# Attention probabilities transposed in 32x32 blocks by VectorE, with 32-row value products

## The chip, the cores and the metric

One Trainium2 chip, one of its cores. The core has TensorE (matmuls, PE in the profile; its weight loads are PEld), VectorE (DVE), ScalarE (ACT), GpSimd (POOL) and SyncE (SP, which only starts transfers). Each engine works through its own queue in order and waits on semaphores. The metric is the device time of one execution in microseconds, the median of several runs; less is better.

## What is computed

One layer of an encoder on 512 positions of width 1024: a gated feed-forward half step, a mixing step, a second feed-forward half step, and a last norm. The change lies in the mixing step:

```
h = rms_norm(x, mix_norm);  u = h @ w_in        # 512 fourier | 8x64 q | 2x64 k | 2x64 v
A = real(fft2(fourier group)) @ fnet_w + fnet_b # per group of 128 channels
q, k = rms_norm per head, then axial rotary
p = softmax(q @ k.T / 8)                        # 4 query heads share one k, v head
B = p @ v
x = x + concat([A, B]) @ w_out
```

All values are float32. The kernel gets this precision from TensorE's faster format (fp32r) by splitting each operand into a high part (a rounded copy) and a low part (value minus high part), and adds three products: high x high, high x low, low x high (`product`, L163 to L166).

## The kernel before

Activations lie with channels on partitions and the 512 positions along the free axis, in 8 tiles of 128x512. The mixing stage is written as some 600 small named operations (`op`), and one long list, `ORDER`, says in which order they are issued; each engine's queue is the list's operations that fall to it. The names that matter here, with t = 0..3 the query pair, b = 0, 1 the key/value head, c a block of 128 queries, kc a block of 128 keys:

- `w*.r/.h/.l`, `f*.`, `fw.`, `o*.`: a weight tile is loaded by SyncE (r), ScalarE makes its high part (h, L858) and VectorE its low part (l, L123, `lows`). f0 to f3 belong to the Fourier projection, o0 to o7 to the output projection. `HI_DVE` names those whose high part VectorE makes (f0, f1).
- `k.0..7`, `q0.0..7`, `v.0..7`: steps of the projections, three 512-column products each; `n1.*` is the row scale of the norm (L233; n1.t turns it on TensorE), `.rc/.rs` the rotary, `.pq/.s0/.s1/.s2` the per-head scale in `sc` (s1 on GpSimd, L949).
- `s{t}{b}{c}` scores (L1188, L1189), `m` the row maximum by a reduce and a multiply on VectorE (L1194, L1195), `e` the exponentials on ScalarE with their row sum (L1202).
- `t{t}{b}{kc}` turns the probabilities: four 128x128 transposes on TensorE into one PSUM bank (L1214). `h` (ScalarE, L1219) and `l` (VectorE, L123) split the bank into high and low part, tiles ph and pl. `v` multiplies them with the values (L1257, tile `vst`: high and low part of v side by side, 128 columns). The rows of high and low part are then added (`o.c` L1267 on ScalarE, `o.a` L1272 on VectorE).
- `z.r/.w/.p` invert the row sums, spread them (GpSimd, L1239) and turn them on TensorE; `r.m/.h/.l` scale the result and split it. `y{d}.0..7` are the eight steps of output block d; k = 0..3 take the Fourier part, k = 4..7 the attention part.
- `f{h}{c}.`, `d`, `c`, `map`: the Fourier mixer.

PSUM has 8 banks of 128x512. In the mixing stage `bank_for` hands them out in turn, and `read` gives one back after its last reader.

Of the kernel before, what the change touches and what calls it, by code (L numbers as in the profile page):

```python
# [13 lines left out]
P = 128  # L14
# [23 lines left out]
HI_DVE = ("f0", "f1")  # L38
# [5 lines left out]
wk.r wq0.r wv.r cos wk.h wk.l wq0.h k.0 k.1 k.2 k.3 k.4 wv.h k.5 wq0.l k.6 wq1.r k.7 k.sq q0.0 wq1.h n1.c  # L44
k.rc n1.m k.sw n1.p q0.1 q0.2 q0.3 q0.4 wq1.l q0.5 wq2.r n1.t q0.6 q0.7 wq2.h q1.0 k.rs k.pq wv.l q0.sw
n1.b v.0 v.1 k.s0 k.s1 wq2.l q0.rc f2.r wq3.r q0.rs q0.ah q0.bh k.s2 v.2 kw v.3 v.4 v.5 v.6 q0.sq q0.al
q0.bl v.7 vt kp wq3.h km q1.1 wq3.l q0.pq f0.r q0.s0 k1.0 k0.0 k0.1 q1.2 q1.3 q1.4 q1.5 k1.2 k0.2 vp q1.6
q1.7 k0.3 s003 s001 s000 k1.1 k1.3 s010 f1.r v0.h v0.l q0.s1 q0.s2 f0.h m001 m003 s002 q1.sw m002 m010 q1.sq
q1.sd q1.pq e002 m000 v1.h e000 e001 e003 q2.0 q2.1 q2.2 q1.s0 q1.s1 f0.l q1.rc q1.rs v1.l q2.3 q2.4 q1.bh
q2.5 q2.6 q2.7 q2.sw t001 e010 f1.h f1.l q2.rc t000 q3.0 s012 h000 l000 s011 m011 t002 h002 h001 m012 q1.ah  # L50
q1.al q2.sq q3.1 q3.2 q3.3 q3.4 q3.5 q3.6 q1.bl q3.7 s013 l002 e011 v000 e012 f2.h l001 v001 q2.sd q3.sw
q2.rs t003 m013 q2.ah q3.rc q3.sq v002 e013 q2.bh f2.l s100 q1.s2 m100 s102 h003 q3.sd e100 f00.0 t010 f3.r
q2.bl h010 q2.pq l003 q2.s0 q2.s1 t013 m102 e102 s101 m101 f00.1 f00.u q2.al v003 l010 e101 t011 h011 q3.rs
s103 t012 f02.0 h013 l011 z0.r o00.c o00.a q3.bh v010 v011 m103 h012 l012 q3.pq q3.s0 l013 e103 s110 m110
s201 q3.ah s111 q3.bl v012 v013 o01.c t100 m111 h100 l100 e111 o0.r t101 h101 t102 h102 o01.a fw.r f02.1
e110 s112 m112 e112 z0.w pos q2.s2 l102 f01.0 s113 l101 z0.p m113 e113 s203 r0.m f02.e s200 m200 v100 v101
t103 t110 f01.1 r0.h h103 l103 z1.r f02.h v102 f01.u e200 q3.al q3.s1 v103 o10.c t112 m201 h110 r0.l h112
s202 m202 l110 t113 m203 f03.0 f03.1 v110 f3.h q3.s2 o10.a e201 s210 f03.e f3.l t111 l112 f10.0 f02.l h113
h111 l111 e202 f10.1 f03.h e203 s211 v111 m210 o2.r fw.h e210 t200 h200 t202 l113 m211 v112 s300 l200 v113
h202 t201 f10.u h201 l202 o11.c s212 m212 e212 s213 z1.w e211 f12.0 fw.l l201 f12.1 m300 e300 m213 e213  # L60
o11.a z1.p r1.m s301 v200 t203 r1.h f03.l h203 f12.e l203 f12.h z2.r z2.w v201 v202 t211 s302 m302 t210 h210
l210 s303 m303 h211 l211 v203 o20.c o20.a t212 h212 m301 f11.0 f13.0 e302 s311 l212 f12.l o0.h o0.l r1.l
t213 f11.1 f11.u m311 v210 v211 f13.1 h213 l213 f13.e e303 v212 s310 d00 m310 e301 t302 o1.r o1.h o1.l t301
f13.h f13.l e310 v213 o21.c t300 o21.a h302 l302 map0 map0.h map0.l d10 h300 l300 map1 z2.p d00.h map1.h
d00.l e311 t303 r2.m map1.l h303 l303 v300 s312 h301 m312 d20 d01 o2.h s313 d11 l301 v301 v302 v303 m313
e312 d01.h d01.l c0.s o2.l e313 t312 d11.h d11.l o30.c d31 o30.a h312 l312 o4.r c0.c c0.q c0.o t311 d10.h
t310 h311 h310 l310 d10.l d20.h d21 d20.l l311 c0.h c0.l d30 t313 c1.c d21.h d21.l o3.r c1.s c1.q d30.h v310
c1.o d31.h d31.l v311 v312 y1.0 h313 l313 c2.s z3.r z3.w c1.h o6.r d30.l c2.q c2.c y0.0 c2.o c2.h y2.0 c3.s
c3.q v313 r2.h c1.l z3.p c2.l c3.c c3.o y1.1 y2.1 y2.2 y0.1 r2.l y0.2 c3.h c3.l y2.3 y0.3 y1.2 y0.4 y0.5
y0.6 o31.c o31.a r3.m r3.h y1.3 y1.4 r3.l y0.7 o3.h y1.5 y2.4 y0.x y2.5 y2.6 o3.l y1.6 o5.r y1.7 o4.h y0.q  # L70
o4.l y1.x y1.q y2.7 o5.h o5.l y3.0 y1.a y3.1 y3.2 y3.3 y3.4 y3.5 y3.6 y3.7 y1.h o6.h o6.l y3.x y3.q y4.0
y4.1 y4.2 y2.x y2.q y4.3 y5.0 y4.4 y4.5 y4.6 y3.h y3.l o7.r y5.1 y5.2 y5.3 y4.7 y4.x y4.h y2.a y3.a o7.h
y6.0 o7.l y0.h y5.4 y5.5 y4.l y5.6 y4.q y4.a y5.7 y6.1 y6.2 y0.l y6.3 y6.4 y5.x y7.0 y6.5 y2.h y6.6 y6.7
y6.x y1.l y2.l y7.1 y6.q y7.2 y7.3 y7.4 y7.5 y7.6 y5.q y7.7 y6.h y6.l y5.h y5.l y5.a y7.x y7.q y6.a y7.h
y7.a y7.l
# [8 lines left out]
def encoder(ctx, tc, A, out):  # L84
# [15 lines left out]
    pp = ctx.enter_context(tc.tile_pool(name="psum", bufs=8, space=bass.MemoryType.PSUM))  # L100

    def bank(name):
        return pp.tile([P, S], F32, tag="bank", name=name)
# [18 lines left out]
    def lows(lo, src, hi):  # L122
        nc.vector.tensor_tensor(out=lo, in0=src, in1=asf(hi), op=ALU.subtract)  # L123
# [44 lines left out]
    class Norm:  # L168


        def __init__(self, n):
            self.n = n
            self.acc = tp.tile([P, S], F32, tag="acc", name=f"acc{n}")
            self.r = cp.tile([P, 4], F32, name=f"r{n}")
            self.ms = cp.tile([P, 4], F32, name=f"ms{n}")
            self.rb = cp.tile([P, S], F32, tag="rb", bufs=2, name=f"rb{n}")

# [71 lines left out]
    def ffn(norm, after, wgu, wd, wdt, groups, opening, closing):  # L249
# [6 lines left out]
        with tc.tile_pool(name=f"act{n_}", bufs=1) as ap, tc.tile_pool(name=f"sums{n_}", bufs=2) as sp:  # L256
            room(ap, 192)
# [546 lines left out]
    n2 = Norm(2)  # L804
    with tc.tile_pool(name="mix", bufs=1) as mp, tc.tile_pool(name="mixt", bufs=1) as mt:

        room(mp, 192)
# [5 lines left out]
        def temp(name):  # L813
            return mt.tile([P, S], F32, tag="t", bufs=9, name=name)

        cos = mp.tile([P, S], F32, name="cos")
        sin = mp.tile([P, S], F32, name="sin")
        chan = mp.tile([P, 4, P], F32R, name="chan")
        pos = mp.tile([P, 2, 2, 514], F32R, name="pos")
        odd = mp.tile([P, 258], F32R, name="odd")  # L820
        sc = mp.tile([P, 4, 10], F32, name="sc")
        room(mp, 32)
# [13 lines left out]
        spare, held = [bank(f"mix{i}") for i in range(8)], {}  # L836

        def bank_for(name, readers=1):
            held[name] = [spare.pop(0), readers]
            return held[name][0]  # L840

        def read(name):
            held[name][1] -= 1
            if not held[name][1]:
                spare.append(held.pop(name)[0])

# [3 lines left out]
        def weight_ops(name, src, n=KD):  # L850
# [29 lines left out]
        def rope_ops(name, g):  # L880
# [3 lines left out]
            @op(f"{name}.sq")  # L884
            def _():
                sqs[name] = mt.tile([P, S], F32, tag="sqm", bufs=3, name=f"sq_{name}")
                nc.scalar.activation(sqs[name], banks[name], AF.Square)
                read(name)

            @op(f"{name}.sw")  # L890
            def _():
                swaps[name] = sw = tp.tile([P, S], F32, tag="g", name=f"sw_{name}")
                if by_dma:
                    owns[name] = mt.tile([P, S], F32, tag="own", name=f"own_{name}")
# [62 lines left out]
        def query_ops(t):  # L957
# [3 lines left out]
            @op(f"{name}.ah")  # L961
            def _():
                qa[t] = mp.tile([P, S], F32R, name=f"qa{t}")
                nc.scalar.copy(qa[t][0:HD], rots[name][0:HD])
# [6 lines left out]
            def _():  # L971
                qb[t] = mp.tile([P, S], F32R, name=f"qb{t}")
# [36 lines left out]
        vst = mp.tile([P, 2, 4, 2, HD], F32R, name="vst")  # L1009
# [601 lines left out]
```

## Time and profile before

| | |
|---|---|
| median of 3 runs | 837.93 us (837.79 to 838.09) |
| profiled execution | 837.96 us, span 836.2 us |
| granted TensorE clock | 0.999 |
| mixing stage on TensorE | 335.6 to 497.2 us of the span |
| weight load (LDWEIGHTS) of 128x128 | 188 ns, under the matmul before it |
| four-transpose groups of probabilities | 32, of 128x128 each four times |
| value products, 128x512 | 64 |

The profile lists groups of equal instructions by line, engine and tiles, with their number, busy time in us, mean ns of one, and the idle time before them with what ended it. The window view gives the busy time of each engine in a stretch. The chain of waits follows the work that ended last backwards; its rows are start and length, which for TensorE is the distance to the next matmul's start. Times count from the span's start.

### The profile page before, as it was taken

To read this page: it belongs to the slowest core of one execution; us is meant where nothing else is said; L and a number is where in the kernel's file an instruction comes from. 1 tells how busy PE (TensorE), PEld (TensorE's weight loads), DVE (VectorE), ACT (ScalarE), POOL (GpSimd) and SP (SyncE) were. 2 spreads that over 40 slices of the span, in tenths; PEclk is the share of its full clock that TensorE was granted. 3 is DMA by queue.
4 is the path that set the end of the run, shared out by engine and by line. 5 is a ranking of instruction groups with operands and counts; after the bars stand their busy time and mean duration, and the time that the engine had idled before them with its cause. 6 is when DMAs were issued, how large, how long until landed. Compare 5 with 4: busy or idle time off the path is not lost.

```text
span 836.2 us, 13649 instructions
## 1 busy us (share of the span) xinstructions
PE 829.4 (99%) x5418; PEld 752.3 (90%) x5418; DVE 603.4 (72%) x923; ACT 461.9 (55%) x770; POOL 62.5 (7%) x69
## 2 busy tenths in 40 slices
PE   9999999999999999999999999999999999999997
PEld 7888998899989998889999888899988999899986
DVE  7977884578656867699999478878755885578563
ACT  7654763366434644677776446546533663356452
POOL 0111000000000000222000000110000000000001
PEclk9999999999999999999999999999999999999999
DMA  7787765468365423414020326777554674456122
GB/s 253 189 199 191 199 187 147 117 159 226 97 169 151 121 58 114 151 51 146 26 76 26 100 57 170 187 182 197 165 154 125 179 206 131 116 167 189 45 78 101
DMA packets 46110, 117.16 MB, mean 140 GB/s; under 512 B 5216, under 2 KB 9952, under 8 KB 45920
## 3 DMA queue, kind: packets, MB, share of 16 engines
q1 hardware_dynamic: 38128, 92.57, 33.5%
q0 software_dynamic: 7648, 23.47, 16.4%
q8 instruction: 42, 0.69, 0.3%
q10 hardware_dynamic: 272, 0.26, 0.1%
q14 instruction: 20, 0.16, 0.1%
HBM read 111.83 MB, written 2.10 MB: 136 GB/s over the span
## 4 chain that ended last, share of the span: by engine, by line
PE 99%; issue 0%; DVE 0%; POOLq 0%; POOL 0%; ACT 0%
PE r L429 23%; PE q L429 11%; PE dn L166 9%; PE dn L164 9%; PE dn L165 9%; PE p L429 6%; PE mix L164 4%; PE mix L166 3%; PE mix L165 3%; PE gu L766 3%; PE gu L164 3%; PE gu L165 3%; PE gu L166 3%; PE mix L1257 2%; PE mix L1214 2%; PE mix L1188 1%
## 5 line engine op out<-in xcount | busy, mean ns | idle before, releaser
L429 PE MATMUL r<-rt,ring 128*128 128x256 f32 x1686 | 204.9, 276 | 0.0
L429 PEld LDWEIGHTS r<-rt,ring 128*128 128x128 f32 x1686 | 198.5, 188 | 0.9
L165 PE MATMUL dn<-at,ring 128*128 128x512 f32 x295 | 114.8, 389 | 0.0
L166 PE MATMUL dn<-at,ring 128*128 128x512 f32 x295 | 114.8, 389 | 0.0
L164 PE MATMUL dn<-at,ring 128*128 128x512 f32 x295 | 114.8, 389 | 0.0
L429 PE MATMUL q<-rt,ring 128*128 128x256 f32 x840 | 106.6, 276 | 0.0
L374 ACT CAST ring<-s 128x1024 fp32r<-128x1024 f32 x70 | 73.5, 1050 | 58.3 <-DVE s L394 51.5
L581 DVE SCALAR_TENSOR_TENSOR gx<-dn,gx 128x512 f32<-128x512 f32 x61 | 42.1, 691 | 81.1 <-PE dn L166 81.1
L429 PEld LDWEIGHTS q<-rt,ring 128*128 128x128 f32 x840 | 100.4, 188 | 0.0
L123 DVE TENSOR_TENSOR ring<-s,ring 128x1024 fp32r<-128x1024 f32 x70 | 85.3, 1219 | 0.6 <-ACT ring L374 0.6
L156 ACT CAST ring<-raw_dn 128x768 fp32r<-128x768 f32 (+2 forms) x48 | 40.7, 852 | 75.6 <-PE dn L165 70.5
L166 PEld LDWEIGHTS dn<-at,ring 128*128 128x128 f32 x295 | 55.4, 188 | 11.5
L165 PEld LDWEIGHTS dn<-at,ring 128*128 128x128 f32 x295 | 55.4, 188 | 11.1
L164 PEld LDWEIGHTS dn<-at,ring 128*128 128x128 f32 x295 | 55.4, 188 | 11.0
L346 POOL DMA_DIRECT2D s<-in_wgu x35 | 30.1, 861 | 423.5 <-DVE ring L123 146.7
L429 PE MATMUL p<-rt,ring 128*128 128x256 f32 x420 | 53.3, 276 | 0.0
L123 DVE TENSOR_TENSOR ring<-raw_dn,ring 128x768 fp32r<-128x768 f32 (+2 forms) x48 | 46.7, 977 | 7.1 <-ACT ring L156 7.1
L429 PEld LDWEIGHTS p<-rt,ring 128*128 128x128 f32 x420 | 50.2, 188 | 0.0
L123 DVE TENSOR_TENSOR ring<-raw_g,ring 128x1024 fp32r<-128x1024 f32 x35 | 42.6, 1217 | 0.0
L123 DVE TENSOR_TENSOR at<-u,at 128x512 fp32r<-128x512 f32 x35 | 24.2, 693 | 20.3 <-ACT at L484 20.2
L472 DVE TENSOR_TENSOR u<-g,u 128x512 f32<-128x512 f32 x35 | 24.0, 687 | 19.8 <-ACT u L469 19.8
L374 ACT CAST ring<-raw_g 128x1024 fp32r<-128x1024 f32 x35 | 36.8, 1051 | 0.0
(312 smaller groups left out, 1523.0 us busy)
## 6 DMA issues: line engine op xcount, KB each, us to landing
s<-in_wgu SPq DMA_DIRECT2D x70, 256.0 KB, 4.2
s<-in_wgu POOLq DMA_DIRECT2D x35, 512.0 KB, 5.7
raw_g<-in_wgu SPq DMA_DIRECT2D x35, 512.0 KB, 4.0
raw_dn<-in_wd SPq DMA_DIRECT2D x44, 384.0 KB, 3.9
raw_u<-in_wgu SPq DMA_DIRECT2D x35, 256.0 KB, 4.1
raw_gu<-in_wgu SPq DMA_DIRECT2D x12, 512.0 KB, 3.5
raw_o<-in_wo SPq DMA_DIRECT2D x8, 512.0 KB, 3.6
raw_dn<-in_wd SPq DMA_DIRECT2D x5, 448.0 KB, 4.2
```

What stands on the lines that cost most here:

```text
L123: nc.vector.tensor_tensor(out=lo, in0=src, in1=asf(hi), op=ALU.subtract)
L156: nc.scalar.copy(hi[:, :n, :], raw[:, :n, :])
L164: nc.tensor.matmul(ps, whi, mhi, start=first, stop=False)
L165: nc.tensor.matmul(ps, whi, mlo, start=False, stop=False)
L166: nc.tensor.matmul(ps, wlo, mhi, start=False, stop=last)
L346: nc.gpsimd.dma_start(out=blocks(t), in_=up, accum_op=ALU.add)
L374: nc.scalar.copy(ts[0], src)
L429: nc.tensor.matmul(ps[:, c], a[:, ks], b[:, i, c], start=first and i == 0 and o == 0, stop=i == KH - 1 and o == 2, skip_group_check=not fi ...
L472: nc.vector.tensor_tensor(out=self["u"], in0=self["g"], in1=self["u"], op=ALU.mult)
L581: nc.vector.scalar_tensor_tensor(out=x[d][:, t], in0=ps[:, t], scalar=0.5, in1=x[d][:, t], op0=ALU.mult, op1=ALU.add)
L766: nc.tensor.matmul(pss[c], w[:, k % 2, c], m[k], start=k == 0 and m is hh and w is hi, stop=k == KD - 1 and w is lo,)
L1214: nc.tensor.transpose(pts[n][:, c * P : (c + 1) * P], prob[t, b, c][:, kc * P : (kc + 1) * P], ident)
```

## The change

The probabilities are no longer turned on TensorE. VectorE transposes each 128x512 tile of exponentials in blocks of 32x32 (`x`, L1264 of the new kernel), which leaves the four query strips of 32 in the partitions and, within a block, keys and queries exchanged. High and low part go into one buffer `its` for a set of eight items (two query pairs, four query blocks, one key/value head); GpSimd makes 26 of the 32 low parts. A product now contracts over 32 rows: `p{st}` issues, for each of the 16 key strips j, both parts and each of the four partition strips a, one matmul of 32 rows, 128 columns of weights and 256 columns (8 items x 32 queries), strip a into bank a of a four-bank tile `quad`. The values must therefore stand in every strip: 32 transfers from GpSimd's queue (`vr`) write them four times into `vrep`. There are four sets, with one buffer.

Further: the maximum is one TENSOR_SCALAR with an accumulator, in place in PSUM; the values get the norm's scale after their turn (`vm`), so n1.t and n1.b are gone; twelve weights (f0 to f3, o0 to o7) get their low part as a negated copy of the high part by ScalarE (`.n`) and a transfer from GpSimd's queue that adds the weights to it; wq1, wq2, wq3, wv and fw get theirs from GpSimd; z0 and z1 are spread by ScalarE; tiles share room (`early`, `late`). `ORDER` is new. The rows of `w_out` are in their plain order.

```diff
+LOWS_POOL = """
+000 002 003 010 011 013 100 101 102 111 112 113 200 201 202 203 210 212 213 300 301 302 303 310 311 312 fw wq1 wq2
+wq3 wv
+LOWS_DMA = """
+o0 o1 o2 o3 o4 o5 o6 o7 f0 f1 f2 f3
...
 ORDER = """
-wk.r wq0.r wv.r cos wk.h wk.l wq0.h k.0 k.1 k.2 k.3 k.4 wv.h k.5 wq0.l k.6 wq1.r k.7 k.sq q0.0 wq1.h n1.c
+wk.r wq0.r wv.r cos wk.h wk.l wq0.h k.0 k.1 k.2 k.3 k.4 wv.h k.5 wq0.l k.6 wq1.r k.7 k.sq q0.0 wq1.h n1.c q0.1 wq2.r
...
+            if name in LOWS_DMA:
+                op(f"{name}.n")(lambda: nc.scalar.activation(ws[name][1], asf(ws[name][0]), AF.Copy, scale=-1.0))
+                op(f"{name}.l")(lambda: nc.gpsimd.dma_start(out=ws[name][1], in_=src, accum_op=ALU.add))
+                return
...
+            def spread(a):
+                for i in range(4):
+                    src, dst = slice(32 * i, 32 * i + 32), slice(32 * a, 32 * a + 32)
+                    nc.gpsimd.dma_start(
+                        out=vrep[dst].rearrange("p (c i) e -> p c i e", i=4)[:, :, i],
+                        in_=stage[v][src].rearrange("p c o e -> p c (o e)"),
+                    )
...
-                nc.vector.tensor_reduce(out=mx, in_=sps[n], axis=AX.X, op=ALU.max, negate=True)
-                nc.vector.tensor_tensor(out=mx, in0=mx, in1=f, op=ALU.mult)
+                nc.vector.tensor_scalar(
+                    out=sps[n], in0=sps[n], scalar1=f, scalar2=None, op0=ALU.mult, op1=ALU.min, accum_out=mx
+                )
...
-                    nc.tensor.transpose(pts[n][:, c * P : (c + 1) * P], prob[t, b, c][:, kc * P : (kc + 1) * P], ident)
+                nc.vector.transpose(turned[n], probs[n])
+            op(f"h{n}")(lambda: (nc.vector.tensor_copy if n in HI_DVE else nc.scalar.copy)(ph, turned[n]))
+            op(f"l{n}")(lambda: lows(pl, turned[n], ph, nc.gpsimd if n in LOWS_POOL else nc.vector))
...
+                all_quads(f"p{st}", 4)
+                for j in range(16):
+                    for o in range(2):
+                        for a in range(4):
+                            rows = slice(32 * a, 32 * a + 32)
+                            nc.tensor.matmul(
+                                quad[:, a, : 8 * 32], vrep[rows, j], its[rows, o, :, 32 * j : 32 * j + 32],
+                                start=j == 0 and o == 0, stop=j == 15 and o == 1, skip_group_check=True,
+                            )
...
-                for i, p in enumerate(parts[n]):
-                    nc.tensor.matmul(outs[t, b], w, p, start=kc == 0 and i == 0, stop=kc == 3 and i == 1)
```

How the instructions move. TensorE before, in the middle of the stage (ks, qa: scores; ph, pl, vst: value products; ident, e: transposes of probabilities; mix: PSUM banks):

```order
L1188 MATMUL mix_3414<-ks_3418,qa_3825 128x512
L1189 MATMUL mix_3414<-ks_3419,qa_3825 128x512
L1257 MATMUL mix_3415<-ph_4003,vst 128x512
L1257 MATMUL mix_3415<-pl_4005,vst 128x512
L1257 MATMUL mix_3415<-ph_4015,vst 128x512
L1257 MATMUL mix_3415<-pl_4069,vst 128x512
L1214 MATMUL mix_3416<-ident,e_3853 128x128
L1214 MATMUL mix_3416<-ident,e_3919 128x128
L1214 MATMUL mix_3416<-ident,e_3893 128x128
L1214 MATMUL mix_3416<-ident,e_3977 128x128
```

and now, around the third set (L1240, L1241 are the scores, L178 to L180 the Fourier products, its and vrep the operands of the 32-row products):

```order
L1240 MATMUL bank_70<-ks_3315,qb_3335 128x512
L1241 MATMUL bank_70<-ks_3316,qb_3335 128x512
L1240 MATMUL bank_73<-ks_3315,qb_3335 128x512
L1241 MATMUL bank_73<-ks_3316,qb_3335 128x512
L1279 MATMUL quad<-its,vrep 128x256 x128
L178 MATMUL bank_72<-ring 128x256
L179 MATMUL bank_72<-ring 128x256
```

Transposes and value products, spread in small pieces between the scores, have become one block of 128 matmuls that stands at four places of the queue.

VectorE before, in the same part (mx: maxima; pl: low parts; oo: the sum of high and low rows):

```order
L1194 TENSOR_REDUCE mx112_4042<-mix0_3409 128x1
L1195 TENSOR_TENSOR mx112_4042<-mx112_4042,sc_3407 128x1
L953 SCALAR_TENSOR_TENSOR sc_3407<-sc_3407,r1_91 128x4x2
L123 TENSOR_TENSOR pl102_4053<-mix5_3414,ph102_4021 128x512
L123 TENSOR_TENSOR pl101_4069<-mix6_3415,ph101_4015 128x512
L1194 TENSOR_REDUCE mx113_4075<-mix7_3416 128x1
L1195 TENSOR_TENSOR mx113_4075<-mx113_4075,sc_3407 128x1
L1278 TENSOR_TENSOR oo0_3952<-mix4_3413,oo0_3952 128x512
```

and now, shortly before the third set (x: block transposes, el and fo: Fourier parts):

```order
L1246 TENSOR_SCALAR bank0_70,mx313_4584<-bank0_70,sc_3336 128x512
L1246 TENSOR_SCALAR bank1_71,mx312_4590<-bank1_71,sc_3336 128x512
L1264 STREAM_TRANSPOSE x213_4592<-e213_4521 128x512
L137 TENSOR_TENSOR ring_61<-bank2_72,ring_61 128x255
L1246 TENSOR_SCALAR bank3_73,mx311_4727<-bank3_73,sc_3336 128x512
L1264 STREAM_TRANSPOSE x210_4732<-e210_4581 128x512
L137 TENSOR_TENSOR el00_3324<-fo0_4558,eh00_3320 128x512
L1264 STREAM_TRANSPOSE x310_4745<-e310_4575 128x512
```

The place of the low parts has been taken by the transposes; most low parts stand in GpSimd's queue. That queue before, over the whole stage:

```order
L949 TENSOR_TENSOR sc<-sc,mhalf 128x4x2
L1239 COPY zw_4297<-z_3852 128x512
L1239 COPY zw_4364<-z_4126 128x512
L1239 COPY zw_4733<-z_4331 128x512
L233 TENSOR_TENSOR r_3391<-ms_3392,mhalf 128x4
```

and now, in the last third of it (L886: adding transfers of output weights):

```order
L137 TENSOR_TENSOR its<-x_4490,its 128x512
L886 DMA ring<-in_wo 128x1024
L1313 COPY zw_4753<-zall 128x512
L886 DMA more<-in_wo 128x1024
L886 DMA ring<-in_wo 128x1024
L137 TENSOR_TENSOR its<-x_4592,its 128x512
L137 TENSOR_TENSOR its<-x_4732,its 128x512
L137 TENSOR_TENSOR its<-x_4745,its 128x512
L137 TENSOR_TENSOR its<-x_4757,its 128x512
L137 TENSOR_TENSOR its<-x_4803,its 128x512
```

GpSimd's queue went from a few small operations to low parts, value copies and adding transfers in one order.

More of the change, by code (lines that the diff above doesn't have):

```diff
@@ L811, in encoder @@
         plain.extend(more)
[L813 to L822, printed above, removed]
+        region = {"tag": "region", "bufs": 1}
+        early = mp.tile([P, 6, S], F32, name="early", **region)
+        cos, sin, own = early[:, 0], early[:, 1], early[:, 5]
+        late = {}
         ops = {}
@@ L833, in op @@
             return put
-        spare, held = [bank(f"mix{i}") for i in range(8)], {}
+        spare, held = [(b, any(b is q for q in quads)) for b in turn], {}
         def bank_for(name, readers=1):
-            held[name] = [spare.pop(0), readers]
-            return held[name][0]
+            i = next((i for i, b in enumerate(spare) if not b[1]), 0)
+            held[name] = [spare.pop(i), readers]
+            return held[name][0][0]
         def read(name):
@@ L1284, in output_ops @@
+            op(f"r{st}.l")(lambda: lows((qa, qb)[b][first + 1], pair[st], (qa, qb)[b][first]))
         def output_ops(d):
@@ L1352, in encoder @@
         op("n1.p")(lambda: n1.power(0, 4))
-        @op("n1.t")
-        def _():
-            banks["rp"] = bank_for("rp")
-            for c in range(4):
-                n1.turn(banks["rp"], c)
-        @op("n1.b")
-        def _():
-            nc.scalar.copy(n1.rb, banks["rp"])
-            read("rp")
         @op("pos")
         def _():
-            for t, n in ((chan, "chan"), (pos, "pos"), (odd, "odd")):
-                nc.gpsimd.dma_start(out=t, in_=A[n])
+            t = mp.tile([P, 6 * S], F32R, name="late", **region)
+            a = 0
+            for n, k in (("chan", 4 * P), ("pos", 4 * 514), ("odd", 258)):
+                late[n] = t[:, a : a + k]
+                a += k
+                nc.gpsimd.dma_start(out=late[n], in_=A[n])
         with tc.manual_schedule(engines=ORDERED):
@@ L1558, in _layout @@
     v = np.arange(1152, 1280)
-    mix = np.concatenate([np.arange(512)] + [512 + h * HD + np.arange(HD) for t in range(4) for h in (t, t + 4)])
     x = np.concatenate(
```

266 lines of the change are left out of this document (145 added, 121 removed).

## The prediction

> **What bounds the kernel now.** I read the page first (busy times, then the chain that ended last), then the waits of TensorE, then the middle of the program cut into three stretches.
>
> ```profile
> PE 829.4 (99%) x5418; PEld 752.3 (90%) x5418; DVE 603.4 (72%) x923; ACT 461.9 (55%) x770; POOL 62.5 (7%) x69
> PE 99%; issue 0%; DVE 0%; POOLq 0%; POOL 0%; ACT 0%
> PE busy L705 <- DVE halves L735: 1.0, 1, 1.0
> ```
>
> TensorE sets the end: 99% of the chain, and its only wait is 1.0 us at the start. So a matmul removed is time gained, as long as nothing else takes TensorE's place. All of the change lies in the mixing stage, which TensorE runs from 335.6 to 497.2 us. I cut it at the last query product (378.0) and at the first product of output block 0, y0.0 (452.9).
>
> ```profile
> 335.60:378.00 42.40, 42.40 (x215) 35.63 (x214) 34.75 (x64) 29.61 (x51) 9.12 (x4) 1.00 0.30 100
> 378.00:452.90 74.90, 74.90 (x533) 68.72 (x532) 70.59 (x149) 59.03 (x123) 7.20 (x8) 1.00 0.23 77
> 452.90:497.20 44.30, 44.30 (x202) 36.76 (x202) 26.34 (x40) 18.07 (x27) 0.62 (x1) 1.00 0.23 72
> ```
>
> The columns are length, then busy TensorE, weight loads, VectorE, ScalarE, GpSimd, clock, DMA. The middle row decides: TensorE is full, but VectorE is busy 70.6 of 74.9 us (94%). Work taken from TensorE there shortens the stretch only as far as VectorE's work shrinks too.
>
> **TensorE's terms.** The chain of waits gives start-to-start prices.
>
> ```profile
> 378.64 0.91 PE mix L1257 x4
> 379.55 0.44 PE mix L1214 x4
> ...
> 553.06 1.36 PE q L429 x12
> ```
>
> A value product (128x512) costs 0.91/4 = 0.227 us, four transposes of probabilities 0.44, a 256-column product 1.36/12 = 0.113. Removed: 32 groups of four transposes, 14.1; 64 value products, 14.5; the four transposes of n1.t, 0.44; together 29.1 us. Added: four sets of 128 products of 32 rows by 256 columns. If the four row strips run side by side, a set is 32 rounds of 0.113 = 3.6 us and all four 14.5; if each waits for the one before, 128 x 0.113 = 14.5 a set and 57.9 in all. The trace has no matmul of fewer than 128 rows, so nothing in it decides. I take 3.6: the strips read other partitions and write other banks, and break-even is at 29.1/128 = 0.227 us a round, twice the best case. TensorE alone then gains 14.6 us.
>
> By place (names counted in the two orders; an output step of three 512 products is 0.68, a score pair 0.455, a Fourier channel step 3 x 0.118, a sum over head rows 0.81 by the rows under the second rival): up to the last query product, -3 transpose groups, -n1.t, +1 score, +1 sum = -0.5. In the middle, which now ends at the last set p3, -29 transpose groups (12.8), -31 value products (14.1), +3 sets (10.9), +8 output steps (5.4), +0.7 channel steps, -0.5 score, -0.8 sum = -11.1, leaving 63.8 of 74.9. After that, -8 output steps, -0.7, -0.5, + one set = -3.0.
>
> **VectorE's term, the one that decides.** Groups of lines of the middle stretch, then two rows from a wider window, where one shows how closely independent operations follow.
>
> ```profile
> L123 DVE TENSOR_TENSOR pl<-mix,ph 128x512 fp32r<-128x512 f32 x30 | 20.4, 685 | 0.9 <-ACT ph L1219 0.6
> L1194 DVE TENSOR_REDUCE mx<-mix 128x1 f32<-128x512 f32 x25 | 17.0, 681 | 1.2 <-PE mix L1189 1.1
> L1195 DVE TENSOR_TENSOR mx<-mx,sc 128x1 f32<-128x1 f32 x25 | 4.0, 161 | 0.9
> L1272 DVE TENSOR_TENSOR oo<-mix,oo 64x512 f32<-64x512 f32 x7 | 4.7, 673 | 0.4 <-ACT oo L1267 0.3
> L1171 DVE SCALAR_TENSOR_TENSOR fo<-mix,fb,fq 128x255 f32<-128x255 f32 x4 | 1.7, 474 | 0.0
> L123 DVE TENSOR_TENSOR ring<-raw_o,ring 128x1024 fp32r<-128x1024 f32 x2 | 2.4, 1222 | 0.0
> L123 DVE TENSOR_TENSOR more<-raw_f,more 128x1024 fp32r<-128x1024 f32 x1 | 1.2, 1218 | 0.0
> L123 DVE TENSOR_TENSOR ring<-raw_fw,ring 128x512 fp32r<-128x512 f32 x1 | 0.7, 684 | 0.0
> ...
> L987 DVE COPY kw<-sc 128x512 f32<-128x512 f32 x1 | 0.4, 427 | 0.0
> ...
> 376.85 1.29 DVE L123 TENSOR_TENSOR pl<-mix,ph 128x512 fp32r<-128x512 f32 x2
> ```
>
> Leaving the middle: 30 low parts of probabilities 20.4, five low parts of weights of 1.22 (two f, three o) 6.1, fw 0.7, one output sum 0.7: 27.8 us. Coming: six low parts that stay on VectorE 4.1, three high parts as SBUF copies 3 x 0.43 = 1.3, two channel low parts and one channel output 1.4 + 1.2, one more maximum 0.8, and 29 block transposes. The new maximum (one TENSOR_SCALAR with an accumulator) replaces reduce and multiply: same elements, one instruction more or less, taken as equal. A transpose has no row. Bounds: 0.43, if it ran like the copy; 1.22, if each element took two of the clocks that the 1024-element row shows. I take 0.62, close to the 1.29 - 0.685 = 0.605 at which independent 512-element operations follow each other; 29 x 0.62 = 18.0. Coming together 26.8, so VectorE needs 70.6 - 27.8 + 26.8 = 69.6 us, against TensorE's 63.8. **VectorE becomes the bound of the middle.** It lasts 69.6 if VectorE never idles and 69.6 x 74.9/70.6 = 73.8 at today's share; I take the middle, 71.7, a gain of 3.2 and not 11.1. TensorE will stand before p0 to p3: each set waits for eight finished items and four free banks, the next scores queue behind it, and so the next maxima come late as well.
>
> **ScalarE and GpSimd.**
>
> ```profile
> L1219 ACT CAST ph<-mix 128x512 fp32r<-128x512 f32 x29 | 16.4, 588 | 2.4 <-PE mix L1214 2.0
> L1089 ACT CAST eh<-fe 128x512 fp32r<-128x512 f32 x4 | 2.5, 625 | 0.3 <-DVE fe L1084 0.3
> L858 ACT CAST ring<-raw_f 128x1024 fp32r<-128x1024 f32 x1 | 1.1, 1052 | 0.6 <-PE mix L1064 0.6
> ...
> L346 POOL DMA_DIRECT2D s<-in_wgu x35 | 30.1, 861 | 423.5 <-DVE ring L123 146.7 <-DMA s<-in_wgu 95.4 <-DVE gx L581 50.5
> L1390 POOL TENSOR_TENSOR gx<-gx,rb 128x256 f32<-128x256 f32 x2 | 1.5, 744 | 2.4 <-ACT rb L246 2.4
> L1369 POOL DMA_DIRECT2D chan<-in_chan x1 | 0.6, 616 | 0.0
> ...
> raw_o<-in_wo SPq DMA_DIRECT2D x8, 512.0 KB, 3.6
> raw_f<-in_winf SPq DMA_DIRECT2D x4, 512.0 KB, 3.5
> ```
>
> ScalarE in the middle: 59.0 - 29 x 0.588 + 26 x 0.625 + five negated copies of 1.05 + two spread sums of 0.62 + 1.0 of small ones = 65.6 us: hidden, with little room. GpSimd goes from 7.2 to 24 low parts at 1.3 (between 0.74, the 256-element row, and twice that), 24 copies of values at 0.6, six adding transfers at 0.86, 2.1 of the rest: 53 us. It is in order and sits on the path: between p1 and p2 it must issue 16 value copies (9.6) and six low parts (7.8), 17.4 us, while TensorE has 15.6 of other work. The 12 adding transfers lie a whole block ahead of their products; without that cover each would cost its transfer, some 4 us (the 512 KB f and o loads land in 3.5 and 3.6 us). They read 6 MB of weights a second time, with the DMA engines busy 0.23 of the stage. SyncE issues the same loads, and a raw tile of these 12 is free once ScalarE has read it.
>
> GpSimd and VectorE also disturb each other:
>
> ```profile
> 367.28 1.22 DVE L123 TENSOR_TENSOR ring<-raw_f,ring 128x1024 fp32r<-128x1024 f32 x1
> 367.45 2.54 POOL L949 TENSOR_TENSOR sc<-sc,mhalf 128x8 f32<-128x8 f32 x1 [6.33 <-DVE sc L945]
> 392.36 1.67 POOL L949 TENSOR_TENSOR sc<-sc,mhalf 128x8 f32<-128x8 f32 x1
> ```
>
> The same small operation lasts 2.54 us where a VectorE subtraction of two SBUF tiles was running as it began, 1.67 where none was. Here GpSimd waits. Whether VectorE waits for a long GpSimd operation no row shows. The middle has 25 VectorE operations that could meet one (22 with two SBUF inputs, three copies); GpSimd's arithmetic fills 33 of 72 us, so at random 25 x 0.46 x half of 1.3 = 7.5 us, from below 0. I take 2.2.
>
> Sum against the profiled execution: 837.96 (its span 836.2 and 1.8 around it) - 0.5 - 3.2 - 3.0 + 2.2 = **833.4 us**. The median of the three runs, 837.93, is the same within 0.03.
>
> **Rivals.** *TensorE stays the bound.* A transpose at 0.43 brings VectorE to 64.1, TensorE's 63.8: all 14.6 come, 823.4. For it: the copy row; against it: every other VectorE row of 512 elements is at 0.68.
>
> *The 32-row products queue (slower).* Its mechanism is the weight load: each of the 512 loads 128 columns for only 256 of work.
>
> ```profile
> 348.61 0.95 PE L935 MATMUL mix<-halves,sq_k 128*128 128x2 f32 x8
> 349.42 0.49 PE L164 MATMUL mix<-ring,more 128*128 128x512 f32 x1
> ```
>
> Two-column products still take (349.42 - 348.61)/8 = 0.101 us each: a load has this floor. If loads of different strips don't overlap, a set is 13 to 14.5 us and TensorE's sum is +28.9: 866.9. It decides from 0.227 us a round. [...]
>
> *VectorE and GpSimd hold each other (same or slower).* The full 7.5 us, and GpSimd late by 2 at each of four sets: 838.0 - 6.7 + 7.5 + 8 = 846.8. It decides from 6.7 us of such waits. For it: the 2.54 row, and 17.4 against 15.6 before p2. [...]
>
> [...]
>
> **Chances.** Forecast 0.42 (own range 828 to 837), TensorE bound 0.12, lock 0.20, slow transpose 0.08, queued products 0.18. The range 823 to 850 holds all but the last. 0.2% is 1.7 us, about what this measurement can tell. Faster: 0.40 + 0.12 = 0.52; same: 0.02 + 0.07 of the lock case = 0.09; slower: 0.13 + 0.08 + 0.18 = 0.39.
>
> **What would show it.** A set p should last 3.6 us by the chain; 5 is harmless, 14 is the second rival. STREAM_TRANSPOSE should read near 0.68 and follow within 0.62. The waits of TensorE should now list p0 to p3 with some 8 us in all, ended by VectorE or GpSimd's low parts; VectorE should be over 95% busy between the last query product and p3. [...] The feed-forward stages should keep their times; any change there makes the account wrong, as would TensorE waiting for an adding transfer's low part.

## The result and the profile after

The changed kernel takes 960.95 us (median of 4 runs, 959.18 to 966.15) against 837.86 beside it: ratio 1.148, 95% interval 1.143 to 1.153. It is slower by 123 us, and the forecast of 833.4 was wrong, far outside its range of 823 to 850.

The page of the changed kernel, busy times and the shares of the chain that ended last:

```profile
span 964.4 us, 14468 instructions
...
PE 867.8 (90%) x5734; PEld 760.2 (79%) x5734; DVE 604.7 (63%) x914; ACT 472.3 (49%) x782; POOL 132.3 (14%) x142
...
PE 71%; DVE 13%; issue 6%; ACT 5%; DMA 3%; POOL 1%; SPq 0%; DVEq 0%; POOLq 0%; ACTq 0%
```

TensorE was idle for 836.2 - 829.4 = 6.8 us; now it is idle for 96.6, and busy for 38.4 us more (what makes up this part was not separated). Where, the window view tells. I cut the span where TensorE begins the mixing stage, after the last query product, after the last set p3 and where it begins the second feed-forward stage (columns as in the prediction):

```profile
0.00:385.67 385.67, 351.48 (x2189) 307.36 (x2189) 240.14 (x344) 180.97 (x291) 22.15 (x29) 1.00 0.51 140
385.67:436.60 50.93, 46.45 (x209) 37.13 (x207) 34.95 (x55) 29.42 (x46) 26.95 (x24) 0.93 0.42 109
436.60:530.40 93.80, 79.48 (x887) 70.57 (x886) 78.63 (x162) 66.12 (x138) 55.57 (x59) 0.91 0.50 109
530.40:571.40 41.00, 38.98 (x173) 31.14 (x170) 16.81 (x24) 20.84 (x27) 4.31 (x5) 1.00 0.62 141
571.40:964.40 393.00, 351.38 (x2285) 314.00 (x2283) 234.18 (x330) 175.01 (x282) 23.33 (x27) 0.99 0.47 128
```

Stage lengths in us. The forecast's middle ended at the start of p3; here p3 with its 3.6 us is counted into the middle.

| stage | before | forecast | after | e4 | e9 |
|---|---|---|---|---|---|
| first feed-forward | 335.6 | 335.6 | 385.7 | 335.6 | 336.1 |
| mixing, head | 42.4 | 41.9 | 50.9 | 49.1 | 46.3 |
| mixing, middle | 74.9 | 75.3 | 93.8 | 84.6 | 85.5 |
| mixing, tail | 44.5 | 37.9 | 41.0 | 42.4 | 39.1 |
| second feed-forward, to the span's end | 338.8 | 338.8 | 393.0 | 342.7 | 339.7 |

(e4 and e9 are experiments below. In the forecast, 2.2 us for VectorE and GpSimd stand in no stage.) A stage is read from the one profiled execution of each kernel. The two feed-forward stages, in which nothing was to happen, lost 50.1 and 54.2 us: four fifths of the loss. Four groups of the page show how (last columns: busy us, mean ns, idle us before them and what ended most of it):

```profile
L447 PE MATMUL quad<-rt,ring 128*128 128x256 f32 x1516 | 202.4, 283 | 36.2 <-ACT p L455 14.0
L447 PE MATMUL bank<-rt,ring 128*128 128x256 f32 x1430 | 173.7, 277 | 0.0
L178 PE MATMUL quad<-at,ring 128*128 128x512 f32 x157 | 63.0, 401 | 20.1 <-DVE gx L599 14.7
L179 PE MATMUL bank<-at,ring 128*128 128x512 f32 x138 | 53.7, 389 | 0.0
```

The same matmul, on the same line, waits for 36.2 us where it writes `quad` and never where it writes `bank`. `quad` is the four-bank tile that the 32-row products write; outside the mixing stage its banks are handed out in turn like the others. One place in the timeline of the changed kernel (start, length, what; in brackets the idle time before and what ended it):

```profile
319.85 1.58 PE L447 MATMUL quad<-rt,ring 128*128 128x256 f32 x12
...
321.46 0.37 ACT L455 COPY u<-quad 128x256 f32<-128x256 f32 x1 [0.56 <-PE quad L447]
...
321.88 1.65 PE L447 MATMUL quad<-rt,ring 128*128 128x256 f32 x12 [0.46 <-ACT u L455]
...
323.37 1.52 PE L447 MATMUL bank<-rt,ring 128*128 128x256 f32 x12
323.57 0.39 ACT L487 ACTIVATE u<-quad 128x256 f32<-128x256 f32 x1 [1.74 <-PE quad L447]
```

A group of twelve fills one bank of the tile; ScalarE copies it out; only then does the group for the next bank of the tile begin. The third group, into a bank with a tile of its own, starts while the second is still being read. So a product into one bank of the joined tile seems to wait for the readers of the others. That was the theory for the experiments (A).

### The profile page after: what moved, and what is told of

It reads as the page before. It is cut to its first block, busy times and chain, and to the rows that moved or that the text cites. A ratio compares the mean times of both kernels' runs of the same rounds, so it can differ in the third digit from the quotient of the medians.

```text
span 964.4 us, 14468 instructions
## 1 busy us (share of the span) xinstructions
PE 867.8 (90%) x5734; PEld 760.2 (79%) x5734; DVE 604.7 (63%) x914; ACT 472.3 (49%) x782; POOL 132.3 (14%) x142
## 4 chain that ended last, share of the span: by engine, by line
PE 71%; DVE 13%; issue 6%; ACT 5%; DMA 3%; POOL 1%; SPq 0%; DVEq 0%; POOLq 0%; ACTq 0%
PE quad L447 19%; PE bank L447 15%; PE bank L178 6%; PE bank L179 6%; PE bank L180 6%; PE quad L178 5%; PE quad L180 5%; PE quad L179 5%; DVE gx L599 2%; DVE ring L137 2%; ACT p L455 1%; DMA more<-in_wo 1%; DVE x L1264 1%; PE bank L1472 1%; DMA raw_first<-in_first 1%
## 5 line engine op out<-in xcount | busy, mean ns | idle before, releaser
L447 PE MATMUL quad<-rt,ring 128*128 128x256 f32 x1516 | 202.4, 283 | 36.2 <-ACT p L455 14.0
L447 PEld LDWEIGHTS quad<-rt,ring 128*128 128x128 f32 x1516 | 184.1, 188 | 50.4 <-ACT p L455 19.6
L447 PE MATMUL bank<-rt,ring 128*128 128x256 f32 x1430 | 173.7, 277 | 0.0
L447 PEld LDWEIGHTS bank<-rt,ring 128*128 128x128 f32 x1430 | 168.5, 188 | 0.2
L178 PE MATMUL quad<-at,ring 128*128 128x512 f32 x157 | 63.0, 401 | 20.1 <-DVE gx L599 14.7
L599 DVE SCALAR_TENSOR_TENSOR gx<-quad,gx 128x512 f32<-128x512 f32 x32 | 22.1, 691 | 69.8 <-PE quad L180 69.8
L179 PE MATMUL quad<-at,ring 128*128 128x512 f32 x157 | 61.2, 390 | 0.0
L180 PE MATMUL quad<-at,ring 128*128 128x512 f32 x157 | 61.1, 389 | 0.0
L178 PEld LDWEIGHTS quad<-at,ring 128*128 128x128 f32 x157 | 29.4, 188 | 34.1 <-ACT ring L170 12.7
L179 PE MATMUL bank<-at,ring 128*128 128x512 f32 x138 | 53.7, 389 | 0.0
L180 PE MATMUL bank<-at,ring 128*128 128x512 f32 x138 | 53.7, 389 | 0.0
L178 PE MATMUL bank<-at,ring 128*128 128x512 f32 x138 | 53.7, 389 | 0.0
L599 DVE SCALAR_TENSOR_TENSOR gx<-bank,gx 128x512 f32<-128x512 f32 x29 | 20.0, 692 | 38.6 <-PE bank L180 38.6
L137 POOL TENSOR_TENSOR its<-x,its 128x512 fp32r<-128x512 f32 x26 | 35.1, 1393 | 12.8 <-ACT its L1266 10.7
```

What stands on the lines that cost most here:

```text
L137: (by or nc.vector).tensor_tensor(out=lo, in0=src, in1=asf(hi), op=ALU.subtract)
L178: nc.tensor.matmul(ps, whi, mhi, start=first, stop=False)
L179: nc.tensor.matmul(ps, whi, mlo, start=False, stop=False)
L180: nc.tensor.matmul(ps, wlo, mhi, start=False, stop=last)
L447: nc.tensor.matmul(ps[:, c], a[:, ks], b[:, i, c], start=first and i == 0 and o == 0, stop=i == KH - 1 and o == 2, skip_group_check=not fi ...
L599: nc.vector.scalar_tensor_tensor(out=x[d][:, t], in0=ps[:, t], scalar=0.5, in1=x[d][:, t], op0=ALU.mult, op1=ALU.add)
```

## The experiments

**What the joined tile does alone.** e1 is the kernel before with nothing but the change's banks:

```diff
-    pp = ctx.enter_context(tc.tile_pool(name="psum", bufs=8, space=bass.MemoryType.PSUM))
+    pp = ctx.enter_context(tc.tile_pool(name="psum", bufs=1, space=bass.MemoryType.PSUM))
+    quad = pp.tile([P, 4, S], F32, name="quad")
+    quads = [quad[:, i] for i in range(4)]
+    singles = [pp.tile([P, S], F32, name=f"bank{i}") for i in range(4)]
+    turn = singles[1:] + quads + singles[:1]
...
-        return pp.tile([P, S], F32, tag="bank", name=name)
+        turn.append(turn.pop(0))
+        return turn[-1]
```

> The kernel before, with one thing of the change: its eight accumulator banks are no longer eight tiles but one tile of four banks and four of one, handed out in the same turn. Theory A (a product into one bank of the four-bank tile waits until the readers of its other banks are done): the two feed-forward stages lose what they lost under the change, 50.0 and 54.1 us, and the mixing stage between 0 and its whole 24.0, so 940 to 965 us, with TensorE idle only ahead of products into the four-bank tile. Rival B (the loss comes from what the change added around the mixing stage: adding transfers, GpSimd, the order): 836 to 840 us.

e2 has the same turn over eight fixed tiles of one bank:

```diff
+    turn = [pp.tile([P, S], F32, name=f"bank{i}") for i in range(8)]
```

> The kernel before, with eight fixed tiles of one bank handed out in turn in place of a pool that rotates eight buffers. Theory A (only the joining of four banks in one tile costs): 836 to 840 us, no wait of TensorE over 2 us in all. Rival C (the loss comes from fixed tiles, which are never released, or from the turn): about 940 us or more, as the change with its joined tile.

Measured: e1 1004.05 us (1002.44 to 1007.06), ratio 1.198 (1.196 to 1.201); e2 838.19 us, ratio 1.000 (0.999 to 1.001), with TensorE's one wait of 1.0 us at the start. Both use all eight banks in a turn; they differ in the joining alone. So the chip's banks are not what is waited for, and theory A holds; rivals B and C fall. TensorE's waits in e1 name the same readers as in the changed kernel:

```profile
PE quad L434 <- ACT p L442: 14.0, 28, 1.0
PE quad L169 <- DVE gx L586: 12.8, 15, 0.9
PE quad L434 <- DVE g L481: 9.9, 15, 1.2
```

The size missed: 166 us, where I had at most 127. The feed-forward stages lost 48.9 and 41.2 (335.6 to 384.5, 338.8 to 380.0), where 50.0 and 54.1 were expected: the first is met, the second is 13 us short. The mixing stage lost 74.5 and not 0 to 24. There the kernel before takes the bank that has been free longest, while the changed one takes a bank of the tile only when no other is (`bank_for`, L851); that this is the difference was not tried.

**The change without the joined tile.** e3 has eight single tiles in the feed-forward stages and the joined one only for the mixing stage. e4 has eight single tiles everywhere and reads the sums of a set bank by bank:

```diff
-    quad = pp.tile([P, 4, S], F32, name="quad")
-    quads = [quad[:, i] for i in range(4)]
+    quads = [pp.tile([P, S], F32, name=f"quad{i}") for i in range(4)]
...
-                o, _, l = halves_of(t)
-                nc.scalar.copy(o, l)
+                for o, _, l in halves_of(t):
+                    nc.scalar.copy(o, l)
```

> The changed kernel, with the four-bank tile only for the mixing stage and eight tiles of one bank in the two feed-forward stages. Theory A: the feed-forward stages return to 335.7 and 338.9 us (within 2 us each), the mixing stage stays near its 185.8, so 855 to 865 us. Rival B (adding transfers, GpSimd, order): the feed-forward stages stay at 385.7 and 393.0, 955 to 965 us.

> The changed kernel with eight tiles of one bank everywhere; the sums of a set are read bank by bank, 32 small ScalarE copies and 32 small VectorE sums in place of eight and eight. Theory A: feed-forward stages at 335.7 and 338.9; the mixing stage loses its waits on the four-bank tile (about 8 us of TensorE's list there, the longest 6.1) and pays about 48 small operations more, some 0.2 to 0.3 us each on two engines, so 845 to 862 us. Rival B: 955 to 965 us. If the mixing stage keeps 185.8 or more, its 24 us have another cause than the joined tile (VectorE and GpSimd, as forecast).

Measured: e3 860.51 us (ratio 1.026, 1.023 to 1.030), feed-forward stages 336.8 and 341.6; e4 855.27 us (1.021, 1.019 to 1.023), stages 335.6 and 342.7. Theory A holds for both, though the second stage keeps 2.8 and 3.9 us; in e4 most of that belongs to its start (e9 below). Of the loss of 123 us the joined tile makes 960.95 - 855.27 = 105.7 (net of the 48 small operations that e4 adds); the rest of the change, 17 us, is another matter. The windows of e4's mixing stage:

```profile
335.57:384.65 49.08, 46.37 (x209) 37.25 (x208) 33.09 (x58) 30.62 (x49) 27.09 (x23) 0.93 0.43 118
384.65:469.29 84.64, 74.81 (x886) 66.64 (x884) 77.07 (x176) 64.86 (x152) 55.55 (x59) 0.96 0.53 118
469.29:511.72 42.43, 39.00 (x174) 31.16 (x170) 17.18 (x30) 21.20 (x33) 4.32 (x5) 1.00 0.63 137
```

VectorE is busy 91% of the middle, as forecast, but for 77.1 us; and the granted clock is 0.93 and 0.96 where it was 1.00.

**The turn.** e7 is the changed kernel, joined tile and all, with single and joined banks alternating:

```diff
-    turn = singles[1:] + quads + singles[:1]
+    turn = [b for two in zip(singles, quads) for b in two]
```

> The changed kernel with its joined four-bank tile everywhere, but the turn alternates a bank of its own with a bank of the joined tile, in all stages where banks go by turn. Theory A (a product into the joined tile waits for readers of its other banks): two products in a row are seldom in the joined tile, so most readers are done when the next comes: the feed-forward stages lose 10 to 50 us where they lost 104, and the whole is 870 to 915 us. Rival G (the joined tile's banks are slow for whatever reason, however they take turns): 945 to 970.

Measured: 921.41 us (918.71 to 928.18). Better by 40 us, so the order of the turn matters and rival G falls, but the feed-forward stages still lose 30.5 and 34.1 us, more than I had expected: TensorE waits in L447 for VectorE's g (11.1 us) and ScalarE's u (7.1 us), readers of an accumulator that lag by more than one product.

**The parts of the change in the mixing stage**, each as an edit of e4.

e5 takes o0 to o7 out of `LOWS_DMA` (VectorE subtracts them again):

> As e4 (no joined tile), but the low parts of the eight output weights are again VectorE subtractions from the raw tile; the four f weights keep the adding transfers. Theory D (adding transfers that land after their product was due stop TensorE): the waits on them, 5.3 us in e4, go with the slow clock behind them, and VectorE's eight added subtractions of 1.22 us fall mostly where it is 40% busy: 847 to 853 us. Rival E (VectorE bounds the middle, the transfers are harmless): up to 8 x 1.22 = 9.8 us come on top of e4's 855.3, 857 to 865.

e6 takes fw, wq1, wq2, wq3 and wv out of `LOWS_POOL`:

> As e4, but the low parts of wq1, wq2, wq3, wv and fw are made by VectorE (1.22 us each by its 1024-element row) and not by GpSimd (2.45 to 2.74 us). Theory F (the head of the mixing stage, 49.1 us against 42.4 before, is late because these low parts are slow on GpSimd or hold VectorE up): the head returns to 43 to 46 us, and the whole to 849 to 853. Rival I (the head is late because the changed order asks for kp and the first scores before VectorE's key chain is done): the head stays at 48.5 to 50.5 and the whole at 854 to 858.

Measured: 853.33 (852.36 to 854.59) and 853.78 us (851.48 to 856.75), each just above what D and F had and below what their rivals had, so neither pair is decided. The gains on e4, 1.9 and 1.5 us, are no larger than the spread of one kernel's runs (e4: 854.25 to 857.54). Two rows of e4's waits are what e5 removes:

```profile
PE bank L179 <- DMA ring<-in_wo: 3.7, 2, 2.6
PE bank L179 <- DMA more<-in_wo: 1.6, 1, 1.6
```

And e4's list of transfers (number, size, median us from issue to landing):

```profile
raw_o<-in_wo SPq DMA_DIRECT2D x8, 512.0 KB, 4.0
ring<-in_wo POOLq DMA_DIRECT2D x5, 512.0 KB, 7.1
more<-in_wo POOLq DMA_DIRECT2D x3, 512.0 KB, 7.5
```

The adding transfer of output weights needs 7.1 to 7.5 us here (5.7 and 6.8 in the changed kernel) where the plain load of the same weights needs 4.0. In e5 those waits are gone and the tail is shorter (42.4 to 39.1), but the middle grows by 2.4 (84.6 to 87.1): where e4 waits 2.6 us for a transfer, e5 waits 4.0 for VectorE's fo. The head is shorter too (49.1 to 46.8), but not by the edit, which changes nothing there. The key step's wait of 1.7 us stands in both heads; behind it e4 has two stretches of 3.4 us at a granted clock of 0.50 and e5 has none (last section). Heads of the kernels made from e4 with the same projections go by their number: 46.8 with none (e5), 47.8 and 47.9 with one (e8, e10), 48.4 and 49.1 with two (e12, e4).

In e6 the head falls to 44.7, in F's range, and the middle grows by 2.9. The wait for kw is gone from its list. Against e5's head, also without such a stretch, the gain is 2.1 us. Both kernels give back in the middle most of what they gain elsewhere.

e8 gives VectorE the 26 low parts of probabilities that GpSimd makes. "The lock", here and among the forecast's chances, is my name for its third rival, VectorE and GpSimd holding each other:

> As e4, but the 26 low parts of probabilities that GpSimd makes are VectorE's too. Theory J (VectorE bounds the middle, and GpSimd's help is worth more than the lock costs): VectorE's 77.1 us of the middle gain 24 x 0.69 = 16.6 and lose some 5 of stretched subtractions, so the middle lasts 90 to 97 us and the whole 861 to 868. Rival H (holding each other and GpSimd's 1.35 us each cost more than they give): the middle at 84 or less, the whole 845 to 855.

Measured: 866.47 us (865.67 to 868.78), middle 96.6: theory J. GpSimd's help is worth 11 us. What it costs shows in the groups of VectorE, first of e4, then of e8:

```profile
L1263 DVE STREAM_TRANSPOSE x<-e 128x512 f32<-128x512 f32 x32 | 21.8, 695 | 0.3 <-ACT e L1254 0.2
L136 DVE TENSOR_TENSOR its<-x,its 128x512 fp32r<-128x512 f32 x6 | 5.9, 995 | 0.1
L951 DVE TENSOR_TENSOR sw_q<-sw_q,early 128x512 f32<-128x512 f32 x4 | 3.9, 978 | 4.1 <-DMA sw_q<-early 3.1 <-ACT sw_q L928 1.0
L952 DVE TENSOR_TENSOR rot_q<-rot_q,sw_q 128x512 f32<-128x512 f32 x4 | 3.7, 934 | 0.1
L136 DVE TENSOR_TENSOR el<-fe,eh 128x512 fp32r<-128x512 f32 x4 | 3.3, 828 | 0.0
```

```profile
L1262 DVE STREAM_TRANSPOSE x<-e 128x512 f32<-128x512 f32 x32 | 22.0, 698 | 0.1
L135 DVE TENSOR_TENSOR its<-x,its 128x512 fp32r<-128x512 f32 x32 | 21.5, 679 | 1.8 <-ACT its L1264 1.8
L951 DVE TENSOR_TENSOR rot_q<-rot_q,sw_q 128x512 f32<-128x512 f32 x4 | 2.8, 692 | 0.1
L950 DVE TENSOR_TENSOR sw_q<-sw_q,early 128x512 f32<-128x512 f32 x4 | 2.7, 682 | 2.2 <-DMA sw_q<-early 1.1 <-ACT sw_q L927 1.0
...
L135 DVE TENSOR_TENSOR el<-fe,eh 128x512 fp32r<-128x512 f32 x4 | 2.6, 662 | 0.0
```

These four groups of VectorE operations with two SBUF inputs average 0.83 to 1.0 us in e4, beside GpSimd's low parts of probabilities, and 0.66 to 0.69 in e8 without them. The transposes, with one input, keep 0.70 us. So VectorE is held up too, but only in some kinds of its operations. An operation with one input can be among them, as a row of e4's middle shows:

```profile
L973 DVE TENSOR_SCALAR sc<-sc 128x8 f32<-128x8 f32 x2 | 1.4, 724 | 0.1
```

This operation has one SBUF input. It takes 0.17 us in e8; of the two here one starts at 398.16, while a low part on GpSimd runs (398.13 to 399.40), and takes 1.27 us.

e10 puts the old maximum back (TENSOR_REDUCE and a small product):

> As e4, with the maximum as before the change: a reduction and a small product, and no write of the scaled scores. If the two forms cost the same, as the forecast had it (0.74 + 0.134 us now, 0.681 + 0.161 before): 25 x 0.03 = 0.8 us less of VectorE's middle, 853 to 856 us. If the rewritten scores hold their bank longer and stop TensorE's next scores: 848 to 852.

Measured: 858.28 us (857.60 to 859.37): 3 us slower than e4, outside both expectations. The small product, again with two SBUF inputs, accounts for it. First e10's two groups, then those of e4's middle:

```profile
L1245 DVE TENSOR_REDUCE mx<-bank 128x1 f32<-128x512 f32 x23 | 15.4, 669 | 0.7 <-PE bank L1240 0.6
L1246 DVE TENSOR_TENSOR mx<-mx,sc 128x1 f32<-128x1 f32 x32 | 12.2, 382 | 1.1
```

```profile
L1245 DVE TENSOR_SCALAR_CACHE_REDUCE bank<-bank,sc 128x512 f32<-128x512 f32 x19 | 13.7, 738 | 0.4
...
L1245 DVE DVE_READ_ACCUMULATOR bank<-bank,sc 128x1 f32 x19 | 2.5, 134 | 0.0
```

The small product took 161 ns before the change and takes 382 now that GpSimd computes. A maximum is 1.05 us in this form and 0.87 in the changed one; over 32 that is 5.8 us of VectorE. The 12 products that overlap GpSimd's arithmetic average 0.75 us, the 20 others 0.16. The new form is a gain in this company.

e12 takes work off VectorE and off nothing else:

```diff
-                nc.vector.transpose(turned[n], probs[n])
+                half = pool.tile([P, S], F32, name=f"x{n}", **how)[:, : S // 2]
+                nc.vector.transpose(half, probs[n][:, : S // 2])
+                turned[n] = half.unsqueeze(1).to_broadcast([P, 2, S // 2])
```

> As e4, but VectorE transposes only the first half of each tile of probabilities, and both halves of the parts are made from it, so the output is not the reference's; every other operation keeps its size. It takes 29 x 0.34 = 10 us of VectorE's work from the middle and nothing from another engine. Theory J (VectorE bounds the middle): 84.6 us become 74 to 79, the whole 844 to 850. Rival K (GpSimd's low parts, ScalarE or TensorE's order set the middle): the middle stays over 82, the whole at 852 to 856.

Measured: 848.93 us (847.70 to 851.05), middle 80.9: between J and K. Its transposes:

```profile
L1263 DVE STREAM_TRANSPOSE x<-e 128x256 f32<-128x256 f32 x32 | 13.3, 430 | 1.3 <-ACT e L1254 1.3
```

The window of its middle and TensorE's longest wait there:

```profile
384.57:465.49 80.92, 73.72 (x887) 65.73 (x885) 67.22 (x176) 64.41 (x152) 55.81 (x60) 0.98 0.58 129
```

```profile
PE bank L179 <- DMA ring<-in_wo: 4.1, 2, 2.9
```

VectorE had 9.9 us less to do and the middle lost 3.7, one stretch at half clock (two in e4's middle, one here) included. What is left is TensorE's 73.7 us of work and 7.2 of waiting, 4.1 of it for adding transfers. With e8 (VectorE busy for 8.6 us more, the middle 12.0 longer) this says that VectorE holds e4's middle up, but with only a few us to the next limit.

**The best that came out.** e9 is e5 and e6 together, with y4.q and y4.a moved ahead of y5.x; e11 moves kp behind v.5, v.6 and q1.4 and gives ScalarE three copies more:

> As e4 with the edits of e5 and e6 together (output weights' and projection weights' low parts on VectorE), and the square and sum of output block 4 moved ahead of block 5's in the order. Theory D and F, each with its own place: e5 gained 1.9 and e6 1.5 us, and the second feed-forward stage, which begins with a wait of 2.0 us for the last sum and runs 336.6 against 332.7 us, gains up to 3.9: 847 to 852 us. Rival J (VectorE bounds the middle and takes back what is given to it): 852 to 857.

> As e9, with TensorE's key step kp three product steps later (v.5, v.6 and q1.4 go ahead of it) and the three high parts of probabilities that VectorE copied given to ScalarE. Theory I (TensorE asks for kp before VectorE has kw): the wait of 1.7 us and the slow clock behind it go, and VectorE's middle loses 1.3 us: 2 to 5 us less than e9. Rival (the key chain's later start moves the first scores by the same): equal to e9 within 1.5.

Measured: e9 849.19 us (ratio 1.013, 1.011 to 1.014), 6.1 less than e4, about the sum of the three edits (1.9 + 1.5, and 3.0 in the second feed-forward stage, whose wait for the last sum fell from 2.0 to 0.6, with no stretch at half clock behind it). e11 849.44, equal to e9 as its rival had it; but e9's list of waits has no wait for kw any more, so there was nothing for e11 to remove, and theory I was not tested. None of the versions of the change is faster than the kernel before. Heads with the same projections differ by 2.3 us in their one profile (above), so that a stage's difference of 1 or 2 us says nothing here.

## Why the prediction was wrong

The step that failed is the sentence "All of the change lies in the mixing stage", and with it "The feed-forward stages should keep their times". The tiles of PSUM are shared by all stages, and the change joins four of them. I had followed `quad` to the four places where it is used on purpose and priced it there ("four free banks"); in the stages without an edit of their own I gave it no price. e1 puts the step at 166 us alone (90 of them in the feed-forward stages), e4 at 105.7 us within the change. None of the rivals held it: the mechanism of each lay in the mixing stage. e1 takes all eight banks in turn, as e2 does, and is 166 us slower, so different banks are not enough where the program's waits go by tile.

The other steps, with e4 as the measure:

- *The bound before, TensorE at 99%*: read rightly from the page; no run takes work from TensorE alone.
- *The 32-row products side by side*: right, and rival two (14 us a set) is out. The term was undersized: the last set in the changed kernel's timeline is 4.05 us from its start to that of the next matmul, where I took 3.6.

```profile
526.33 4.13 PE L1279 MATMUL quad<-its,vrep 32*128 32x256 f32 x128
530.38 0.50 PE L178 MATMUL bank<-eh,more 128*128 128x512 f32 x1
```

At a slower pace it is longer: 114 products of e4's first set stand in its chain of waits with 6.43 us, 0.056 each, right behind a score product that took 0.43 (0.23 at 392.25); the clock of e4's middle is 0.96.

```profile
404.86 6.43 PE quad L1278 x114
```

- *VectorE becomes the bound of the middle*: borne out in the main (91% busy; e8 and e12), but with 77.1 us and not 69.6. The transposes took 0.695 and not 0.62 (29 x 0.075 = 2.2; the slow transpose of the chances, 1.22, is out), the maxima 0.87 and not 0.84 (25 x 0.03 = 0.8), and by the groups of e4 and e8 GpSimd stretched six its by 0.32, four sw by 0.30, four rot by 0.24 and four el by 0.17 (4.8). Together 7.8, against 77.1 - 69.6 = 7.5. That the two are so close is partly luck: left out are e4's own 24 small sums (5.2 us where six of 0.67 were counted), the stretched TENSOR_SCALAR (1.1) and one maximum fewer. "I take 2.2" was too low. No run shows the term: which 25 operations "could meet" one of GpSimd's was an estimate of mine, and the runs showed 4.8 us on these 18. The third rival came true in part, inside the forecast's bound.
- *TensorE will stand before p0 to p3*: not so. e4's list has no wait there; it has 5.2 us before scores (L1239), 5.3 before output steps (L179) and 2.4 before a turn of row sums (L1320).
- *GpSimd's low parts of projection weights* had no price in the head, which was forecast at 41.9 and is 49.1 in e4; with these five on VectorE it is 44.7 (e6). Of these 4.4 us 2.1 remain against e5's head (46.8), which has no stretch at 0.50, as e6's has none; the other 2.3 are what e4's head, with two such stretches, lasts longer than e5's.
- *The adding transfers lie a whole block ahead*: too little. They need 5.7 to 7.5 us and not "some 4", and TensorE waits for them for 5.3 us in e4. Net of VectorE's work that is worth little: e5 is 1.9 us faster, and by the profiles 2.3 us lie in its head, where the edit changes nothing.
- *TensorE's sum falls by 14.6 us*: the instructions are gone, yet e4's page has TensorE as busy as before the change.

```profile
PE 829.4 (97%) x5734; PEld 747.1 (87%) x5734; DVE 599.7 (70%) x938; ACT 473.1 (55%) x806; POOL 132.6 (16%) x142
```

Half of it is the clock, by the windows of e4's head and middle: 0.07 x 49.1 + 0.04 x 84.6 = 6.8 us. That term was missing: I let a wait of TensorE cost its own length.

What stays open: how the 10.5 us by which e9 is slower than the kernel before (849.19 against 838.71 beside it) divide between VectorE in the middle and the slow clock, the other half of TensorE's unchanged busy time, and why e1's mixing stage lost so much.

## What to carry to other kernels

Follow an edit of a shared resource (here the accumulator tiles) through every stage that draws on it, and look there first for a wait, even where no line of the stage changes. Keep accumulators that are handed out in turn in tiles of their own: one strided read over four banks saved some 48 small operations and cost 106 us net. Work given to GpSimd stretched four groups of VectorE's operations with two SBUF inputs here (by 0.17 to 0.32 us each on average), so count such operations ahead of time; transposes were not held (0.70 us in e4 and e8), but one input alone is no safeguard (the TENSOR_SCALAR of L973: 1.27 us against 0.17). And before a gain of 1 or 2 us in a stage is put down to an edit, compare the granted clock of that stage in both profiles.

## What the runs showed of the hardware

A wait of TensorE can cost more than its length. In e4's head the kw wait is followed by a stretch at half pace; rows of its timeline, then two windows (the third number from the end is the granted clock):

```profile
356.56 0.66 PE L1019 MATMUL bank<-ident,kw 128*128 128x128 f32 x4 [1.68 <-DVE kw L1013]
...
358.87 0.62 PE L178 MATMUL bank<-ring,more 128*128 128x512 f32 x1
359.29 0.63 PE L179 MATMUL bank<-ring,more 128*128 128x512 f32 x1
...
362.27 0.41 PE L177 MATMUL bank<-ring 128*128 128x512 f32 x1
```

```profile
355.46:358.87 3.41, 2.31 (x16) 2.15 (x17) 1.77 (x4) 1.10 (x3) 0.56 (x1) 1.00 0.00 0
358.87:362.28 3.41, 3.41 (x10) 2.64 (x9) 1.94 (x6) 0.98 (x2) 2.14 (x1) 0.50 0.00 0
```

From 358.9 to 362.3 products follow each other at 0.43 us and before and after at 0.23: 3.4 us at half the clock, some 1.6 us lost after a wait of 1.68.

Not every wait has this price. In e4 the waits that end at 435.80 (2.44 us), 459.54 (2.60) and 483.43 (1.63) are followed by a clock of 1.00. The same wait can go either way: 2.03 or 2.04 us for the last sum, early in the second feed-forward stage, are followed by 3.4 us at 0.50 in e4, e5, e6 and e10, where the stage lasts 342.7 us, and by none in e8 and e12, where it lasts 341.1. So such a stretch costs 1.6 us there; what decides whether it comes, these runs don't show.

VectorE is held by GpSimd as well as holding it: its went from 0.68 us in e8 to 1.0 in e4, the small product from 0.16 before the change to 0.38 in e10; a small operation of GpSimd took 2.54 us where a VectorE subtraction was running as it began and 1.67 where none was. All these VectorE operations have two SBUF inputs. The transposes, with one, took 0.70 us in e4 and in e8; the TENSOR_SCALAR of L973, also with one, took 1.27 us beside a low part on GpSimd and 0.17 in e8.

That fp32r is TensorE's faster format shows in the kernel before only so far: four float32 transposes of 128 columns stand in its chain with 0.44 us, 0.86 ns a column, an fp32r product of 256 columns with 0.113 us, 0.44 ns a column.
